# Turning the normalised rows by VectorE squares and DMA through DRAM, in a hybrid decoder layer

## The chip, the cores and the metric

The kernel runs on one core of one Trainium2 chip. Five engines work side by side on that core: TensorE (matmuls), VectorE (DVE), ScalarE (ACT), GpSimd (POOL) and SyncE (SP). In this kernel POOL and SP only issue DMAs, apart from some set-up on POOL. The metric is the device time of one execution in microseconds (us). Timings are compared as medians of several runs.

## The reference

One layer of a decoder, for one sequence of 2048 tokens with 1024 channels, all in fp32:

```python
mod = (silu(c) @ w_ada + b_ada)                 # six vectors: sh1, sc1, g1, sh2, sc2, g2
h = x * (1.0 + sc1) + sh1
z = h @ w_in                                    # 1024 -> 2048 columns
y_conv = gate_b * short_conv(gate_c * v_conv)   # causal, 3 taps
y_pool = multiscale_pool(v_pool)                # means over 2, 4, 8, 16 tokens, then a linear map
mix = concat([y_conv, y_pool]) @ w_out
x = layer_norm(ALPHA * x + (1.0 + g1) * mix, ln1_g, ln1_b)
h = x * (1.0 + sc2) + sh2
f = square(relu(h @ w_mlp_in)) @ w_mlp_out      # 1024 -> 4096 -> 1024
x = layer_norm(ALPHA * x + (1.0 + g2) * f, ln2_g, ln2_b)
```

Between the first layer norm and `h @ w_mlp_in` the layout has to change: the layer norm needs a token on a partition and its channels side by side, the matmul needs a channel on a partition and the tokens side by side. This change of layout is what is edited.

## The kernel before

**Arithmetic.** A fp32 matrix is kept as two parts, `hi` (a cast to the matmul's fp32r format, on ScalarE, line 88) and `lo` (the remainder, a subtraction on VectorE, line 89). `split` makes the pair, and `mm3` (lines 93 to 95) multiplies with three matmuls: hi by hi, hi by lo, lo by hi.

**Blocks.** The sequence is done in two blocks of 1024 tokens (b = 0 and 1). Each block goes through input projection, output projection (`out_proj`) and MLP (`mlp`, with `up` and `down`). The projections use a two-by-two block scheme with seven products instead of eight; which sums of blocks go into which product is in the table `ORDER`, and the operands made from the normalised rows are named by it: "11", "21", "22", "1", "2", "3", "4".

**Output projection.** `out_proj` makes eight tiles `R[0]` to `R[7]` of 128 tokens by 1024 channels. A tile starts as rows of `x` (`load_x`, line 875, on POOL's DMA queue), gets matmul results added in (lines 892 and 899), and is then normalised: statistics on ScalarE (`stats_act`), small steps on both engines (`inv_sqrt`), and last `scale` (line 904), which also stores the tile to the DRAM tensor `nsave` (line 906, POOL's queue), from which `residual` reads it later. Tiles 0 to 3 are complete after `matmuls(4, ...)`, tiles 4 to 7 after `matmuls(6, ...)`. A call of `matmuls` over all four tiles is 48 TensorE matmuls of 128x512, and a product of `up` is 24.

**Turning the rows.** `turned(R)` makes the MLP's operands. Its inner function `transposed(h, k0, dst)` turns the tiles of half h (4h to 4h+3) for the two channel blocks k0 and k0+1: four TensorE transposes of 128x128 into one bank of PSUM (line 773), then an affine with the layer norm's gain and bias (already joined with sc2 and sh2) from PSUM into `dst`, on ScalarE (line 778), or for the second channel block of half 1 on VectorE (line 776). `back(step)` calls it:

```python
if h == 0:
    for q in range(4):
        r = transposed(0, 2 * q, t_r())
        nc.gpsimd.dma_start(hsave[q], r)
        operand("11" if q < 2 else "21", q % 2, r)
```

`back(0)` stands between `matmuls(5, ...)` and `matmuls(6, ...)` and makes "11" and "21" from half 0. `back(1)` stands after the first two products of `up` (g = 0) and turns half 1 into raw tiles. `back(2)`, after the first two products of g = 1, splits "22" from them; `back(3)` to `back(6)` make the other four operands, with tiles read back from `hsave`. The MLP thus begins with products that need half 0 alone: "11", "21", again "11", "21" (g = 1), and the fifth product needs "22".

**What sets the order.** The framework gives each engine and each queue one fixed order when the program is built. It follows the order of the code, except where its own model of the work finds a later instruction ready first; `tc.issue_after(...)` adds an order by hand. So an instruction that has to wait on the chip holds up what is behind it on its engine or queue. Buffers are shared by tag: `o` has 10, `w` 6, `r` 5, `h` 28, `ps` (PSUM banks) 8, and a new tile waits until one of its tag is free.

Of the kernel before, what the change touches and what calls it, by code (L numbers as in the profile page):

```python
# [8 lines left out]
F32 = mybir.dt.float32  # L9
F32R = mybir.dt.float32r  # L10
AF = mybir.ActivationFunctionType
ALU = mybir.AluOpType
# [38 lines left out]
def tile_hybrid_layer(ctx: ExitStack, tc: tile.TileContext, opening, xT, x, wada, win,  # L51
# [29 lines left out]
    def t_ps():  # L81
        return mk(pp, [P, H], F32, "ps", 8)
# [4 lines left out]
    def split(src, hi, lo):  # L87
        high = nc.scalar.copy(hi, src)  # L88
        return high.ins, nc.vector.tensor_tensor(lo, src, hi.bitcast(F32), op=ALU.subtract).ins  # L89


    def mm3(ps, whi, wlo, xhi, xlo, first, last, goes_on=False):
        nc.tensor.matmul(ps, whi, xhi, start=first, stop=False, skip_group_check=goes_on)  # L93
# [97 lines left out]
    msum = tc.dram_tile([7, NG - 1, P, H], F32, name="msum")  # L191
    wosum = tc.dram_tile([2, 4, P, T], F32, name="wosum")
    udeep = tc.dram_tile([NC, P, 3 * Q], F32, name="udeep")
    wdeep = tc.dram_tile([NC, P, T + 3 * Q], F32, name="wdeep")

    def ada_first():
# [562 lines left out]
    def turned(R):  # L759
        B = {}  # L760
        raw = []

        def operand(key, q, src):
            hi, lo = t_h(), t_h()
            split(src, hi, lo)
            B[key, q] = hi, lo

        def transposed(h, k0, dst):
            for i in range(2):
                k = k0 + i  # L770
                ps = t_ps()
                for t in range(4):
                    nc.tensor.transpose(ps[:, t * P : t * P + P], R[4 * h + t][:, k * P : k * P + P], ident)  # L773
                sc, sh = lng[:, k : k + 1], lnb[:, k : k + 1]
                if h and i:
                    nc.vector.tensor_scalar(dst[:, i * H : i * H + H], ps, sc, sh, op0=ALU.mult, op1=ALU.add)
                else:
                    nc.scalar.activation(dst[:, i * H : i * H + H], ps, AF.Identity, bias=sh, scale=sc)
            return dst

        def back(h):
# [5 lines that stand above are left out]
            elif h == 1:  # L787
                for q in range(2):
                    raw.append((transposed(1, 4 + 2 * q, t_o()), transposed(1, 2 * q, t_o())))
            elif h == 2:  # L790
                for q in range(2):
                    operand("22", q, raw[q][0])
            elif h == 3:
                for q in range(2):
                    b11 = t_o()
                    nc.sync.dma_start(b11, hsave[q])
                    tt(raw[q][1], raw[q][1], b11, ALU.subtract)
                    operand("1", q, raw[q][1])
                    raw[q] = raw[q][0], raw[q][1], b11
            elif h == 4:  # L800
                for q in range(2):
                    tt(raw[q][0], raw[q][0], raw[q][1], ALU.subtract)
                    operand("2", q, raw[q][0])
            elif h == 5:
                for q in range(2):
                    tt(raw[q][2], raw[q][0], raw[q][2], ALU.subtract)
                    operand("3", q, raw[q][2])
            else:
                for q in range(2):
                    b21 = t_o()  # L810
                    nc.sync.dma_start(b21, hsave[2 + q])
                    tt(b21, b21, raw[q][0], ALU.subtract)
                    operand("4", q, b21)

        return B, back

# [1 line left out]
    class Operands:  # L820
# [10 lines left out]
        def begin(self, n):  # L831
            i = self.index(n)
            r = t_r()
            nc.sync.dma_start(r.rearrange("p (a n) -> p a n", a=2),
                              msum[i, 0:2].rearrange("a p n -> p a n"))
            self.a[n, 0] = parts(r)
            self.weights(n, 0)

        def weights(self, n, g, tile=None):
# [7 lines left out]
        def second(self, n):  # L847
            ns = range(n, min(n + 2, 7))
            r = t_r()
            for i, m in enumerate(ns):  # L850
                self.a[m, 1] = hi, lo = t_h(), t_h()
                nc.sync.dma_start(r[:, halves[i]], msum[self.index(m), 2])
                split(r[:, halves[i]], hi[:, :H], lo[:, :H])

        def third(self, n):
            hi, lo = self.a[n, 1]
            return split(self.mixed[self.index(n)], hi[:, H:], lo[:, H:])

        def whole(self, n):
            self.begin(n)  # L860
# [2 lines left out]
                self.second(n)  # L863
            self.third(n)

    def out_proj(b, ops):
        R, X, Y = [], {}, {}
        B, back = turned(R)
        lo_, hi_ = halves
        mv = {}  # L870
        late, begun = [], []

        def load_x():
            xt = t_o(D)
            nc.gpsimd.dma_start(xt, x[b * T + len(R) * P : b * T + len(R) * P + P, :])
            R.append(xt)

        def matmuls(n, banks, new, ks, then):
# [23 lines left out]
        def scale():  # L902
            t = late.pop()
            begun[:] = [nc.vector.tensor_scalar(R[t], R[t], mv[t][:, 0:1], mv[t][:, 6:7], op0=ALU.add,
                                                op1=ALU.mult).ins]
            nc.gpsimd.dma_start(nsave[t], R[t])

        def normalise(t):
            stats_act(R[t], mv[t])
# [589 lines left out]
```

## Time and profile before

| | |
|---|---|
| median of 3 runs | 1734.65 us (1734.5 to 1736.54) |
| span of the profiled execution, first to last instruction | 1733.2 us |
| TensorE busy (matmul) | 1723.5 us, 99% |
| VectorE busy | 1314.6 us, 76% |
| ScalarE busy | 868.1 us, 50% |
| POOL busy | 205.8 us, 12% |
| bytes moved by DMA | 465.24 MB, mean 268 GB/s |
| TensorE transposes of normalised rows (line 773) | 128 |

The profile is of one execution; its own time is known as the span, and what lies around the span in a timed run is the difference between the two first rows of the table. In the views, a group row reads: line, engine, operation, out<-in with shapes, count | busy time in us, mean ns of one | idle time of the engine just before them, and what ended it. In the time-ordered views a row starts with start time and duration in us; in brackets stands the idle time of the engine before it and what ended it. In the rows of DMA issues stand the size in KB and the median time from issue to landing in us.

### The profile page before, as it was taken

The numbers are of one execution on the slowest core, as the hardware profiler recorded it, in microseconds if no ns is written. First come the engines' busy times: TensorE is split into PE (matmuls) and PEld (weight loads), VectorE is DVE, ScalarE is ACT, GpSimd is POOL, SyncE is SP. The second block draws the span as 40 slices with busy tenths as digits, with TensorE's granted clock in tenths as the row PEclk, the third lists the DMA queues.
The fourth block names the chain that finished last, engine by engine and source line by source line (L and its number), as shares of the span: only waits on it lengthen the run. The fifth ranks groups of instructions, "written<-read, shape, count | busy, mean of one in ns | idle before, by whom it ended". The sixth has DMA issues, their size and how long they took to land.

```text
span 1733.2 us, 21912 instructions
## 1 busy us (share of the span) xinstructions
PE 1723.5 (99%) x7855; PEld 1435.5 (83%) x7855; DVE 1314.6 (76%) x1726; ACT 868.1 (50%) x1172; POOL 205.8 (12%) x399
## 2 busy tenths in 40 slices
PE   9999999999999999999999999999999999999998
PEld 7888888888888888888888888888888889888887
DVE  8897798877777686669686789687566778665896
ACT  6323368554445554446573344775444567444451
POOL 0222220122322000100000000102111110000000
PEclk9999999999999999999999999999999999999999
DMA  9998877778888998887572366657545589777771
GB/s 387 345 337 319 302 267 269 267 262 325 311 326 319 381 418 332 291 286 284 196 271 76 110 219 219 230 185 282 215 179 222 197 290 418 294 273 249 267 264 50
DMA packets 142685, 465.24 MB, mean 268 GB/s; under 512 B 16488, under 2 KB 17008, under 8 KB 142576
## 3 DMA queue, kind: packets, MB, share of 16 engines
q1 hardware_dynamic: 97920, 303.39, 48.0%
q0 software_dynamic: 44656, 160.46, 24.4%
q8 instruction: 61, 1.00, 0.2%
q14 instruction: 48, 0.39, 0.1%
HBM read 318.55 MB, written 145.23 MB: 268 GB/s over the span
## 4 chain that ended last, share of the span: by engine, by line
PE 95%; DMA 3%; issue 1%; DVE 1%; ACT 0%; SPq 0%; POOL 0%; DVEq 0%; POOLq 0%
PE ps L95 30%; PE ps L93 30%; PE ps L94 30%; PE ps L425 3%; DMA r<-in_w 1%; DMA usum<-o 1%; PE ps L773 1%; DVE o L98 0%; DMA o<-in_w 0%; DMA o<-in_opening 0%; DVE w L89 0%; DVE r L98 0%; ACT w L88 0%; DVE o L1369 0%; SPq L108 0%
## 5 line engine op out<-in xcount | busy, mean ns | idle before, releaser
L95 PE MATMUL ps<-h,w 128*128 128x512 f32 x1312 | 510.2, 389 | 0.4 <-DVE w L89 0.4
L94 PE MATMUL ps<-h,w 128*128 128x512 f32 x1312 | 510.3, 389 | 0.0
L93 PE MATMUL ps<-h,w 128*128 128x512 f32 x1312 | 510.0, 389 | 0.0
L93 PE MATMUL ps<-h,h 128*128 128x512 f32 (+1 forms) x1176 | 444.2, 378 | 0.0
L95 PE MATMUL ps<-h,h 128*128 128x512 f32 (+1 forms) x1176 | 444.1, 378 | 0.0
L94 PE MATMUL ps<-h,h 128*128 128x512 f32 (+1 forms) x1176 | 444.0, 378 | 0.0
L88 ACT CAST h<-r 128x1024 fp32r<-128x1024 f32 (+2 forms) x186 | 187.8, 1014 | 298.0 <-PE ps L94 186.8
L95 PEld LDWEIGHTS ps<-h,w 128*128 128x128 f32 x1312 | 246.3, 188 | 52.1 <-DVE w L89 0.8
L94 PEld LDWEIGHTS ps<-h,w 128*128 128x128 f32 x1312 | 246.3, 188 | 51.5 <-DVE h L89 0.5
L93 PEld LDWEIGHTS ps<-h,w 128*128 128x128 f32 x1312 | 246.0, 188 | 51.3 <-ACT h L88 0.2
L89 DVE TENSOR_TENSOR h<-r,h 128x1024 fp32r<-128x1024 f32 (+2 forms) x186 | 217.3, 1173 | 93.5 <-ACT h L88 93.0
L88 ACT CAST w<-r 128x1024 fp32r<-128x1024 f32 x156 | 164.3, 1053 | 242.6 <-PE ps L94 231.3
L89 DVE TENSOR_TENSOR w<-r,w 128x1024 fp32r<-128x1024 f32 x156 | 190.5, 1222 | 96.3 <-ACT w L88 95.4
L94 PEld LDWEIGHTS ps<-h,h 128*128 128x128 f32 x1176 | 221.3, 188 | 41.1
L95 PEld LDWEIGHTS ps<-h,h 128*128 128x128 f32 x1176 | 221.3, 188 | 40.8
L93 PEld LDWEIGHTS ps<-h,h 128*128 128x128 f32 x1176 | 221.3, 188 | 40.5
L98 DVE TENSOR_TENSOR o<-o,o 128x1024 f32<-128x1024 f32 (+2 forms) x193 | 171.1, 890 | 41.0 <-DMA usum<-o 31.8
L98 DVE TENSOR_TENSOR o<-o,ps 128x512 f32<-128x512 f32 (+1 forms) x175 | 113.7, 658 | 54.3 <-PE ps L95 53.4
L89 DVE TENSOR_TENSOR h<-w,h 128x1024 fp32r<-128x1024 f32 x114 | 137.6, 1207 | 4.3 <-ACT h L88 4.1
L88 ACT CAST h<-w 128x1024 fp32r<-128x1024 f32 x114 | 118.6, 1040 | 12.8 <-DMA w<-wdeep 4.1
L1013 POOL DMA_DIRECT2D usum<-o x111 | 59.4, 535 | 472.3 <-ACT o L1010 195.0
L98 DVE TENSOR_TENSOR r<-r,r 128x1024 f32<-128x1024 f32 x60 | 73.4, 1223 | 21.5 <-DMA r<-in_w 17.5
(160 smaller groups left out, 1243.0 us busy)
## 6 DMA issues: line engine op xcount, KB each, us to landing
usum<-o POOLq DMA_DIRECT2D x111, 512.0 KB, 4.8
r<-usum SPq DMA_DIRECT2D x109, 512.0 KB, 5.5
w<-w2sum SPq DMA_DIRECT2D x64, 512.0 KB, 5.9
r<-in_w SPq DMA_DIRECT2D x60, 512.0 KB, 6.0
w<-in_w SPq DMA_DIRECT2D x40, 512.0 KB, 7.4
o<-in_w SPq DMA_DIRECT2D x72, 256.0 KB, 6.4
w2sum<-o POOLq DMA_DIRECT2D x64, 256.0 KB, 6.7
msum<-o POOLq DMA_DIRECT2D x18, 512.0 KB, 4.9
```

The lines of the kernel that those rows point to most:

```text
L88: high = nc.scalar.copy(hi, src)
L89: return high.ins, nc.vector.tensor_tensor(lo, src, hi.bitcast(F32), op=ALU.subtract).ins
L93: nc.tensor.matmul(ps, whi, xhi, start=first, stop=False, skip_group_check=goes_on)
L94: nc.tensor.matmul(ps, whi, xlo, start=False, stop=False, skip_group_check=goes_on)
L95: nc.tensor.matmul(ps, wlo, xhi, start=False, stop=last, skip_group_check=goes_on)
L98: return nc.vector.tensor_tensor(out_, a, b_, op=op)
L425: nc.tensor.matmul(ps[m, h], wt[:, w : w + P], A[k][p // 2][:, hs], start=k == 0 and p == 0, stop=k == KD - 1 and p == 2)
L773: nc.tensor.transpose(ps[:, t * P : t * P + P], R[4 * h + t][:, k * P : k * P + P], ident)
L1013: nc.gpsimd.dma_start(usum[g, i], r)
```

## The change

TensorE transposes no longer turn the normalised rows. `turn(n)` is called by `scale` for each tile, right after its store to `nsave`. It transposes the tile on VectorE: four instructions of 128x256, each of which turns every 32x32 square by itself, into four gathering tiles `blocks` (tag `w` in half 0, tag `o` in half 1). With the fourth tile of a half, each gathering tile is stored to the new DRAM tensor `tsave` by four DMAs of 32 partitions on POOL's queue, in runs of 128 elements, so that the squares come to lie where a full transpose has them. `transposed` then loads two channel blocks from `tsave` by one DMA on POOL's queue and does the affine in place, its first half on ScalarE, its second on VectorE (for both halves of the rows).

For whole runs of tokens to come out of the squares, a tile `R[t]` holds four groups of 32 tokens that lie 128 apart (`rows_of`). So `load_x` and the store to `nsave` are four DMAs of 32 partitions each in place of one, and the left operands of the output projection are split with their tokens in that order (`split_rows`), in pieces of 512 columns: the 1024-wide split in `begin` becomes two.

```diff
--- before.py
+++ after.py
@@ -88,6 +88,17 @@
         high = nc.scalar.copy(hi, src)
         return high.ins, nc.vector.tensor_tensor(lo, src, hi.bitcast(F32), op=ALU.subtract).ins
 
+
+    def by_rows(ap):
+        return ap.rearrange("p (t a j) -> p a t j", t=4, a=4)
+
+    def by_tokens(ap):
+        return ap.rearrange("p (a t j) -> p a t j", t=4, a=4)
+
+    def split_rows(src, hi, lo):
+        for i in range(0, src.shape[-1], H):
+            cs = slice(i, i + H)
+            split(by_tokens(src[:, cs]), by_rows(hi[:, cs]), by_rows(lo[:, cs]))
 
@@ -191,6 +202,7 @@
     udeep = tc.dram_tile([NC, P, 3 * Q], F32, name="udeep")
+    tsave = tc.dram_tile([2, 4, 2, P, H], F32, name="tsave")
     wdeep = tc.dram_tile([NC, P, T + 3 * Q], F32, name="wdeep")
 
@@ -765,17 +777,30 @@
+        blocks = []
+
+        def turn(n):
+            h, t = n // 4, n % 4
+            if t == 0:
+                blocks[:] = [t_o() if h else t_w(F32) for _ in range(4)]
+            for q, r in enumerate(blocks):
+                nc.vector.transpose(r.rearrange("p (b t j) -> p t b j", b=8, t=4)[:, t],
+                                    R[n][:, q * Q : q * Q + Q].rearrange("p (b j) -> p b j", b=8))
+                if t == 3:
+                    for a in range(4):
+                        own = slice(32 * a, 32 * a + 32)
+                        nc.gpsimd.dma_start(
+                            tsave[h, q].rearrange("k (q i) (a r) -> a i (k q) r", q=4, a=4)[a],
+                            r[own].rearrange("i (b r) -> i b r", b=8))
+
         def transposed(h, k0, dst):
-            for i in range(2):
-                k = k0 + i
-                ps = t_ps()
-                for t in range(4):
-                    nc.tensor.transpose(ps[:, t * P : t * P + P], R[4 * h + t][:, k * P : k * P + P], ident)
-                sc, sh = lng[:, k : k + 1], lnb[:, k : k + 1]
-                if h and i:
-                    nc.vector.tensor_scalar(dst[:, i * H : i * H + H], ps, sc, sh, op0=ALU.mult, op1=ALU.add)
+            nc.gpsimd.dma_start(dst.rearrange("p (k n) -> p k n", k=2), tsave[h, k0 // 2].rearrange("k p n -> p k n"))
+            for i, hs in enumerate(halves):
+                sc, sh = (v[:, k0 + i : k0 + i + 1] for v in (lng, lnb))
+                if i:
+                    nc.vector.tensor_scalar(dst[:, hs], dst[:, hs], sc, sh, op0=ALU.mult, op1=ALU.add)
                 else:
-                    nc.scalar.activation(dst[:, i * H : i * H + H], ps, AF.Identity, bias=sh, scale=sc)
+                    nc.scalar.activation(dst[:, hs], dst[:, hs], AF.Identity, bias=sh, scale=sc)
             return dst
 
@@ -833,7 +858,8 @@
-            self.a[n, 0] = parts(r)
+            self.a[n, 0] = hi, lo = t_h(), t_h()
+            split_rows(r, hi, lo)
             self.weights(n, 0)
 
@@ -850,11 +876,11 @@
-                split(r[:, halves[i]], hi[:, :H], lo[:, :H])
+                split_rows(r[:, halves[i]], hi[:, :H], lo[:, :H])
 
         def third(self, n):
             hi, lo = self.a[n, 1]
-            return split(self.mixed[self.index(n)], hi[:, H:], lo[:, H:])
+            return split_rows(self.mixed[self.index(n)], hi[:, H:], lo[:, H:])
 
@@ -863,16 +889,22 @@
+    def rows_of(t):
+        for a in range(4):
+            start = t // 4 * H + a * P + t % 4 * 32
+            yield slice(start, start + 32), slice(32 * a, 32 * a + 32)
+
     def out_proj(b, ops):
         R, X, Y = [], {}, {}
-        B, back = turned(R)
+        B, back, turn = turned(R)
@@
         def load_x():
             xt = t_o(D)
-            nc.gpsimd.dma_start(xt, x[b * T + len(R) * P : b * T + len(R) * P + P, :])
+            for rs, own in rows_of(len(R)):
+                nc.gpsimd.dma_start(xt[own], x[b * T + rs.start : b * T + rs.stop, :])
             R.append(xt)
@@ -903,7 +935,9 @@
             t = late.pop()
             begun[:] = [nc.vector.tensor_scalar(R[t], R[t], mv[t][:, 0:1], mv[t][:, 6:7], op0=ALU.add,
                                                 op1=ALU.mult).ins]
-            nc.gpsimd.dma_start(nsave[t], R[t])
+            for rs, own in rows_of(t):
+                nc.gpsimd.dma_start(nsave[rs.start // P, rs.start % P : rs.start % P + 32], R[t][own])
+            turn(t)
```

More of the change, by code (lines that the diff above doesn't have):

```diff
@@ L813, in back @@
                     operand("4", q, b21)
-        return B, back
+        return B, back, turn
     class Operands:
```

## Prediction

> **What bounds the kernel now.** I read the page first, for shares, then the groups by form, then windows around the output projection, then the time-ordered views of each engine there.
>
> ```profile
> span 1733.2 us, 21912 instructions
> ...
> PE 1723.5 (99%) x7855; PEld 1435.5 (83%) x7855; DVE 1314.6 (76%) x1726; ACT 868.1 (50%) x1172; POOL 205.8 (12%) x399
> ...
> PE 95%; DMA 3%; issue 1%; DVE 1%; ACT 0%; SPq 0%; POOL 0%; DVEq 0%; POOLq 0%
> ```
>
> TensorE is busy for 99% of the span and carries 95% of the chain that ended last. So time taken off TensorE shortens the run, and any new wait of TensorE lengthens it by as much: the other engines have room to follow. The windows below (columns: length, then busy time and count of PE, PEld, DVE, ACT, POOL, then granted clock, DMA share, GB/s) show the two ends of the output projection, block 0 and block 1, and the end of the run.
>
> ```profile
> 235.00:255.00 20.00, 20.00 (x91) 16.56 (x90) 19.35 (x50) 13.00 (x36) 5.97 (x11) 1.00 0.58 226
> ...
> 1097.00:1112.00 15.00, 14.99 (x83) 12.54 (x82) 7.61 (x16) 10.42 (x15) 2.67 (x5) 1.00 0.56 208
> ```
> ```profile
> 1726.00:1731.00 5.00, 0.00 (x0) 0.00 (x0) 4.06 (x9) 1.18 (x4) 0.00 (x0) 1.00 0.36 143
> 1731.00:1733.20 2.20, 0.00 (x0) 0.00 (x0) 0.00 (x0) 0.00 (x0) 0.00 (x0) 0.53 0.41 153
> ```
>
> TensorE never pauses there. VectorE is full in block 0 (19.35 of 20 us) and half idle in block 1 (7.61 of 15): an added VectorE operation delays block 0 by its own length, block 1 hardly.
>
> **What is removed.**
>
> ```profile
> L773 PE MATMUL ps<-ident,o 128*128 128x128 f32 x128 | 15.6, 275 | 0.0
> ```
> ```profile
> 254.86 2.63 PE ps L773 x24
> ...
> 1101.11 2.63 PE ps L773 x24
> ...
> 1126.69 3.54 PE ps L773 x32
> ```
>
> All 128 TensorE transposes go: four runs of 32 (the first of each block is cut in pieces). An uncut run takes 3.54 us on the chain, 0.11 us each, so **-14.2 us** (4 x 3.54). The 275 ns of the group row are the time of one in a pipeline, and the group's union is only 15.6 us. The Trainium skill (TensorE: Matmul & The Clock Gate, Part 4) gives about 275 ns for such a transpose in a kernel; taken as cost it would make 128 x 0.275 = 35 us of gain, an estimate that these rows contradict.
>
> **When the first product of the MLP can start.** Neighbouring matmuls start 0.2267 us apart: the first and last of 197 rows in a row,
>
> ```profile
> 195.76 0.39 PE L94 MATMUL ps<-h,h 128*128 128x512 f32 x1
> ...
> 240.19 0.39 PE L95 MATMUL ps<-h,h 128*128 128x512 f32 x1
> ```
>
> (44.43 / 196). A `matmuls` call of the output projection is 48 of them, 10.9 us; a product of the MLP 24, 5.44 us. Before, the first run of transposes starts when `matmuls(5)` ends (254.9 and 1101.1); then only `matmuls(6)` is left. After, that call ends and product 0 wants operand "11" at 254.9 + 10.9 = 265.8 and at 1101.1 + 10.9 = 1112.0. Product 0 needs the pair of q=0 at once and that of q=1 six matmuls (1.36 us) later: at 267.2 and 1113.4.
>
> **The new chain to it.** It begins when row 3 is scaled (L904).
>
> ```profile
> 239.93 0.69 DVE L892 SCALAR_TENSOR_TENSOR o<-o,ps 128x512 f32<-128x512 f32 x1 [0.37 <-DMA o<-in_x]
> ...
> 254.05 0.81 DVE L904 TENSOR_SCALAR o<-o,mv 128x1024 f32<-128x1024 f32 x1
> ```
> ```profile
> 1090.26 0.69 DVE L899 SCALAR_TENSOR_TENSOR o<-o,ps 128x512 f32<-128x512 f32 x1 [0.46 <-PE ps L95]
> ...
> 1096.02 0.81 DVE L904 TENSOR_SCALAR o<-o,mv 128x1024 f32<-128x1024 f32 x1 [0.97 <-ACT mv L741]
> ```
>
> In block 1 it ends at 1096.8, in block 0 at 254.9, where the transposes of TensorE already waited for it. Then come 4 VectorE transposes, 4 stores to `nsave`, 16 to `tsave` and 4 loads, all these DMAs on POOL's queue, in the order of the code as I read it, then an affine in two halves, a cast and a subtraction for each q.
>
> ```profile
> L89 DVE TENSOR_TENSOR h<-r,h 128x1024 fp32r<-128x1024 f32 x167 | 203.2, 1221 | 93.3 <-ACT h L88 92.8
> ...
> L98 DVE TENSOR_TENSOR o<-o 128x256 f32<-128x256 f32 x40 | 15.9, 419 | 1.1 <-DMA o<-in_w 0.6 <-ACT o L1054 0.3
> ```
> ```profile
> L356 POOL DMA_DIRECT2D msum<-o x18 | 13.0, 721 | 167.4 <-DVE o L276 105.1 <-DVE o L281 36.6 <-DVE o L98 25.2
> ...
> L906 POOL DMA_DIRECT2D nsave<-o x16 | 8.6, 536 | 57.6 <-DVE mv L750 18.4 <-DVE mv L738 15.2 <-DVE o L904 11.0
> ```
> ```profile
> o<-in_x POOLq DMA_DIRECT2D x16, 512.0 KB, 5.6
> nsave<-o POOLq DMA_DIRECT2D x16, 512.0 KB, 4.1
> ```
> ```profile
> L88 ACT CAST h<-r 128x1024 fp32r<-128x1024 f32 x167 | 175.2, 1052 | 290.3 <-PE ps L94 186.0 <-DMA r<-gout 28.7 <-DMA r<-usum 27.0
> ...
> L778 ACT ACTIVATE r<-ps,lnb,lng 128x512 f32<-128x512 f32 x16 | 11.8, 793 | 7.7 <-PE ps L773 7.7
> ```
>
> No row shows a VectorE transpose. 256 elements per partition should cost near the 0.42 us of an addition of that size; bounds 0.2 (L904 moves 1024 in 0.81) and 0.8. POOL's issue takes 0.536 for the 128 rows of `nsave` and 0.721 for `msum`, as many bytes whose 128 rows go as two runs each, 256 runs. A store to `tsave` is 32 x 8 = 256 runs of 512 B, a load of it 128 x 2 runs, so I take 0.72 for both; bounds 0.53 and twice 0.72, since runs this short are in no row of this queue. Landing: 5.6 us for a 512 KB load on this queue, bounds half and twice that. The landing of the stores costs nothing on the path for q=0 and q=1, as the stores of q=2 and q=3 (8 x 0.72 = 5.8 us) are issued over it; were loads put between stores, it would be paid (4.1 us) but 5.8 us of issue would be saved.
>
> The Trainium skill (DMA: Bandwidth & Descriptors, Anatomy of one DMA) fits 2.0 us plus bytes over 436 GB/s, 3.2 us for 512 KB, as an estimate. By it the sum would be 2 x 2.4 = 4.8 us lower; the 5.6 us row is this queue among this kernel's other traffic, and it decides.
>
> Block 1: scaled 1096.8; `nsave` 4 x 0.53 to 1098.9 (the transposes of q=0, 0.4 us, lie under it); 16 stores x 0.72 to 1110.4; loads issued 1110.4 and 1111.1, landed 1116.0 and 1116.7. ScalarE takes 0.79 + 1.05 for each q (the other half of the affine is on VectorE meanwhile): 1117.8 and 1119.7; the subtraction of q=1 (1.22) ends at 1120.9. Wanted at 1113.4: **+7.5 us**. Bounds: 0 and 25.
>
> Block 0: VectorE is full, so the 12 transposes of rows 0 to 2 (12 x 0.42 = 5.0) push the scaling, and the last `x` tile, for which VectorE waited already at 239.93, now comes as four issues (3 x 0.53 = 1.6 later): scaled at 254.9 + 6.6 = 261.5, 6.6 us after `matmuls(5)` ends where block 1 has it 4.3 us before. The same 24.1 us from there (1096.8 to 1120.9) end at 285.6, wanted at 267.2: **+18.4 us**. Bounds: 5 and 36.
>
> Product 1 takes q=2 and q=3. Loads 3 and 4 land within 5 us of the second, and ScalarE needs 1.84 for each; 5.44 us of product 0 cover it: nothing.
>
> **The second half of the rows** ("22", needed four products, 21.8 us, after product 0). Block 1: product 0 at 1112.0 + 7.5 = 1119.5, "22" wanted at 1141.3 and 1142.6. Row 7 should be scaled 6.6 us after `matmuls(6)` (1090.26 to 1096.83 for row 3), at 1118.6; then 2.1 + 11.5 on POOL, 2.1 for four `hsave` stores in between, loads in the order q=2, 0, 3, 1: the third is issued at 1135.8, lands at 1141.4, is split at 1144.5: **+1.9 us** (bounds 0 and 12). Block 0: TensorE comes 11 us later relative to these rows: nothing.
>
> **The clock.** TensorE pauses 5.8 us in one piece in block 1 (1112.0 to the cast of q=0 at 1117.8), 16.7 in block 0. After 5 us without matmuls the clock at the end of the run falls to half (1731, above), and the opening shows what comes after:
>
> ```profile
> L127 PE MATMUL ps<-o 128*128 128x128 f32 x10 | 2.5, 437 | 1.1 <-DVE o L129 1.1
> ...
> L127 PE MATMUL ps<-ident 128*128 128x128 f32 x6 | 0.8, 275 | 0.0
> ```
>
> the first ten last 437 ns, later ones 275. Some 3 us at half speed cost 1.5 us after each long pause: **+3 us** (bounds 0 and 4).
>
> **Edits at no cost.** 12 more issues for `x` and 12 for `nsave` per block (6.4 us each on POOL, 12% busy; covered by POOL's idle time, except where counted). Halving the seven 1024-wide splits of a block adds about 0.15 us each on ScalarE and VectorE, hidden by TensorE's stream; if writes in runs of 32 elements ran at half speed, 28 splits would cost VectorE and ScalarE up to 19 us a block, spread over 100 us where neither is full save block 0's last 20. `turn` holds four of six `w` buffers in the first half, so weights of products 1 and 2 are split later; TensorE waits then anyway.
>
> **Sum:** -14.2 + 7.5 + 18.4 + 1.9 + 3 = +16.6 on 1733.2, which is 1749.8. The median of the runs is 1734.65, 1.45 above the span: **1751.2 us**.
>
> **Rivals.** (1) The waits stay small: loads are put between the stores and issues go at 0.53. Block 0 then loses some 6 us, block 1 about 1, no clock loss: -14.2 + 7 = -7, 1727.5. For it: VectorE half idle in block 1. Against it: 20 issues of 0.53 are 10.6 us alone, and block 1 has 1113.4 - 1096.8 = 16.6 us for them, a load of 3 to 6 us and 3 us of affine and split. 13 in 100.
> (2) The waits eat the saving, 11 to 18 us together: within 0.2% of before (3.5 us, about what can be told from no change). 12 in 100.
> (3) Slower by more, through one fixed order: ScalarE's affines of the first half stand ahead of the statistics of rows 4 to 7. While ScalarE waits for the loads, four rows of statistics (about 6 us) cannot pass, and the second half, covered in my sum, comes 10 us late in each block: 1751 + 20 = 1771. It decides once the loads land later than the framework's model had them. The same size follows if a store of 256 runs takes POOL 1.4 us (2 x 11). For it: each engine's order is fixed before the run. 21 in 100.
> (4) Transposes free 35 us, by the page quoted: 1751 - 21 = 1730. 2 in 100.
> That the transposes stay or were hidden is excluded: the line is gone, and TensorE has no idle time there to hide them.
>
> **Numbers.** Forecast case 52 in 100. The range takes the Pool and landing bounds of (1) and (3): 1729 to 1785; the forecast's own is 1739 to 1765. Faster 0.15, same 0.12, slower 0.73.
>
> **What would show it.** Waits of TensorE on L88/L89 (operands h), of 7 to 8 us near 1110 and 15 to 20 near 265, preceded by waits of ScalarE on a DMA from `tsave`; POOL rows of `tsave` at 0.72 x 64; VectorE transposes of 0.4 us x 64. A first store issue right after L904 but a last one under 9 us later would make me too high; a TensorE wait before product 5 of over 5 us, or `hsave` stores standing in front of the loads, too low.

## The result, and the profile after

The changed kernel takes 1830.43 us (1828.36 to 1831.78) beside 1734.58 us of the kernel before: a ratio of 1.0546, with an interval of 1.0531 to 1.0561. It is 96 us slower where 16.6 us were forecast. The profiled execution has a span of 1830.0 us.

The page of the changed kernel: the span, the busy times, and the chain that ended last.

```profile
span 1830.0 us, 22027 instructions
...
PE 1723.9 (94%) x7727; PEld 1427.4 (78%) x7727; DVE 1339.1 (73%) x1812; ACT 869.2 (47%) x1178; POOL 301.7 (16%) x575
...
PE 62%; DMA 10%; DVE 7%; issue 4%; POOL 2%; ACT 2%; SPq 0%; DVEq 0%; POOLq 0%; ACTq 0%
```

TensorE is as busy as before (1723.9 us against 1723.5, with 128 transposes fewer), but idle for 6% of the span. The chain, 95% TensorE before, now runs 10% through DMAs. The waits of TensorE by line (what for: total, times, longest, all in us):

```profile
PE ps L104 <- ACT w L88: 52.3, 2, 35.7
PE ps L106 <- DVE w L89: 18.6, 5, 8.7
PE ps L104 <- ACT h L88: 17.7, 4, 8.6
PE ps L105 <- DVE h L89: 4.8, 6, 1.5
...
```

The largest waits end on weights (`w`), not on the operands from the rows (`h`). In order of time on TensorE, at the first product of block 0 and then of block 1:

```profile
301.50 0.80 PE L104 MATMUL ps<-h,w 128*128 128x512 f32 x1 [35.67 <-ACT w L88]
...
311.43 0.80 PE L106 MATMUL ps<-h,w 128*128 128x512 f32 x1 [8.71 <-DVE w L89]
...
1188.85 0.80 PE L104 MATMUL ps<-h,w 128*128 128x512 f32 x1 [16.67 <-ACT w L88]
```

The two kernels issue the same 7,727 other matmuls in one order, so the start of the n-th in one trace less that in the other tells how late it is. By stretches:

| stretch | lateness, us | added | the prediction's term |
|---|---|---|---|
| until `matmuls(6)` of block 0 (one run of transposes gone) | 0 to -3.1 | -3.1 | -3.5 |
| first product, block 0 | -3.1 to 42.5 | +45.6 | +18.4 and half of 3 for the clock |
| second run gone | 42.5 to 39.6 | -2.9 | -3.5 |
| second half of the rows, block 0 | 39.6 to 56.1 | +16.5 | 0 |
| until the end of block 1's `matmuls(5)` (x tile late) | 56.1 to 59.6 | +3.5 | 0 |
| third run gone | 59.6 to 57.0 | -2.6 | -3.5 |
| first product, block 1 | 57.0 to 83.8 | +26.8 | +7.5 and half of 3 for the clock |
| fourth run gone | 83.8 to 80.4 | -3.4 | -3.5 |
| second half of the rows, block 1 | 80.4 to 96.1 | +15.7 | +1.9 |
| to the end | 96.1 to 96.7 | +0.6 | 0 |

The gain came as forecast (-12.0, with small waits in it); each new wait is two to eight times its size or was forecast as nothing. What stands in the line to the first wait, on POOL's queue in block 0 of the changed kernel:

```profile
257.19 2.60 POOL L550 DMA_DIRECT2D w<-in_w  x4
...
273.32 0.57 POOL L557 DMA_DIRECT2D w1sum<-w  x1 [13.03 <-DVE w L109]
...
280.38 9.23 POOL L792 DMA_DIRECT2D tsave<-w  x16 [2.20 <-issue]
...
299.71 0.53 POOL L810 DMA_DIRECT2D hsave<-r  x1 [1.23 <-ACT r L803]
300.31 0.72 POOL L797 DMA_DIRECT2D r<-tsave  x1
```

And on VectorE:

```profile
258.33 0.81 DVE L936 TENSOR_SCALAR o<-o,mv 128x1024 f32<-128x1024 f32 x1
...
272.37 0.65 DVE L109 TENSOR_TENSOR w<-w 128x512 f32<-128x512 f32 x1
```

Row 3 is scaled from 258.3 on (the sum had it done at 261.5), and four transposes later, at 260.6, it is turned. But the 16 stores to `tsave` begin at 280.4: POOL holds them behind the stores of the weight sums, which wait 13 us for VectorE's subtractions, and VectorE has these behind the work on rows 4 to 6. The three first loads go out behind them at 289.6; the fourth stands behind three `hsave` stores until 300.3, and the low part of product 0's weights behind its affine (311.43, above).

What the sums add up is itself loaded late: in the kernel before the same four loads went out 32 us earlier.

```profile
225.21 2.21 POOL L538 DMA_DIRECT2D w<-in_w  x4 [1.80 <-DVE w L211]
```

They go into `w` buffers, and the gathering tiles hold four of the six. The loads go out at 225 in each run below that does not turn half 0 on VectorE, at 257 where only half 0 is turned so, and at 248 to 253 in the kernel before with nothing but VectorE's transposes added. No run gives the gathering tiles buffers of their own, so what this alone costs is not measured.

Block 1 has no weight sums there. POOL, then ScalarE:

```profile
1160.78 4.37 POOL L939 DMA_DIRECT2D nsave<-o  x8 [2.66 <-DVE mv L750]
1165.14 9.66 POOL L792 DMA_DIRECT2D tsave<-w  x16
1174.79 2.15 POOL L797 DMA_DIRECT2D r<-tsave  x3
1183.66 0.59 POOL L810 DMA_DIRECT2D hsave<-r  x1 [6.72 <-DVE r L801]
...
1187.66 0.72 POOL L797 DMA_DIRECT2D r<-tsave  x1
...
1197.35 0.56 POOL L810 DMA_DIRECT2D hsave<-r  x1 [7.51 <-ACT r L803]
...
1208.38 2.35 POOL L792 DMA_DIRECT2D tsave<-o  x4
```
```profile
1179.60 0.81 ACT L803 ACTIVATE r<-r,lnb,lng 128x512 f32<-128x512 f32 x1 [0.39 <-DMA r<-tsave]
1183.21 1.04 ACT L88 CAST h<-r 128x1024 fp32r<-128x1024 f32 x1 [2.80 <-DVE r L801]
...
1187.75 1.04 ACT L88 CAST w<-r 128x1024 fp32r<-128x1024 f32 x1
```

The stores take 9.7 us (forecast 11.5) and the first load lands 4.8 us after its issue (5.6). But the cast of the first operand waits 2.8 us for VectorE's half of the affine, and the cast of product 0's weights comes behind three casts of operands, at 1187.8. The fourth load is issued behind the `hsave` stores; the fourth `hsave` store waits until 1197.4, and the stores of the second half, whose rows were turned by 1182.7 (the last four transposes start at 1181.25 and take 1.42), stand behind it and start at 1208.4.

The clock, in the four windows in which it was granted at half:

```profile
270.00:314.40 44.40, 4.20 (x9) 2.92 (x10) 17.81 (x32) 11.83 (x18) 23.18 (x41) 0.50 0.69 223
338.30:348.50 10.20, 4.78 (x10) 2.86 (x11) 3.96 (x6) 5.49 (x7) 1.34 (x2) 0.50 0.82 321
1174.50:1201.80 27.30, 5.04 (x11) 3.59 (x12) 16.55 (x31) 13.49 (x23) 10.74 (x20) 0.50 0.76 259
1225.70:1236.00 10.30, 5.12 (x10) 3.15 (x11) 4.42 (x7) 5.88 (x8) 0.45 (x1) 0.50 0.84 314
```

These are 40 matmuls (the first count of each row). Where nothing else holds them they start 0.43 us apart in place of 0.23: some 8.0 us, within the terms of the table.

### The profile page after: what moved, and what is told of

Its sections match the earlier page's. It is cut to its first block, busy times and chain, and to the rows that moved or that the text cites. A ratio compares the mean times of both kernels' runs of the same rounds, so it can differ in the third digit from the quotient of the medians.

```text
span 1830.0 us, 22027 instructions
## 1 busy us (share of the span) xinstructions
PE 1723.9 (94%) x7727; PEld 1427.4 (78%) x7727; DVE 1339.1 (73%) x1812; ACT 869.2 (47%) x1178; POOL 301.7 (16%) x575
## 3 DMA queue, kind: packets, MB, share of 16 engines
q1 hardware_dynamic: 97920, 303.39, 46.2%
## 4 chain that ended last, share of the span: by engine, by line
PE 62%; DMA 10%; DVE 7%; issue 4%; POOL 2%; ACT 2%; SPq 0%; DVEq 0%; POOLq 0%; ACTq 0%
PE ps L106 21%; PE ps L105 21%; PE ps L104 21%; DVE o L109 2%; DVE h L89 2%; DMA o<-in_w 1%; DMA r<-tsave 1%; DMA tsave<-o 1%; DMA r<-in_w 1%; DMA usum<-o 1%; POOL tsave L792 1%; DMA o<-tsave 1%; DMA nsave<-o 1%; DVE w L89 1%; POOL nsave L939 1%
## 5 line engine op out<-in xcount | busy, mean ns | idle before, releaser
L88 ACT CAST h<-r 128x1024 fp32r<-128x1024 f32 (+1 forms) x200 | 189.1, 955 | 307.7 <-PE ps L105 194.7
L88 ACT CAST w<-r 128x1024 fp32r<-128x1024 f32 x156 | 164.0, 1052 | 259.7 <-PE ps L105 246.8
L89 DVE TENSOR_TENSOR h<-r,h 128x1024 fp32r<-128x1024 f32 (+1 forms) x200 | 218.3, 1101 | 89.8 <-ACT h L88 89.1
L89 DVE TENSOR_TENSOR w<-r,w 128x1024 fp32r<-128x1024 f32 x156 | 190.4, 1221 | 115.1 <-ACT w L88 113.5
L89 DVE TENSOR_TENSOR h<-w,h 128x1024 fp32r<-128x1024 f32 x114 | 137.5, 1206 | 4.8 <-ACT h L88 4.7
L88 ACT CAST h<-w 128x1024 fp32r<-128x1024 f32 x114 | 118.5, 1040 | 14.6 <-DMA w<-in_w 4.9
```

## The experiments

A result without an interval is one timing of that kernel; the four of the changed kernel lie within 3.4 us of one another.

### Which part costs it

Only tiles 0 to 3 turned in the new way (the others by TensorE), only tiles 4 to 7, and none (rows, pieces and splits stay). In these kernels the affine behind TensorE's transposes writes its result in the order of the tokens. The edit for tiles 0 to 3 alone, with `...` for what is left out; the second run has `h == 0` and `t >= 4` in it, the third `True` and no `turn`:

```diff
         def transposed(h, k0, dst):
+            if h == 1:
+                for i, hs in enumerate(halves):
+                    k, ps = k0 + i, t_ps()
+                    for t in range(4):
+                        nc.tensor.transpose(ps[:, t * P : t * P + P], R[4 * h + t][:, k * P : k * P + P], ident)
+                    sc, sh = (v[:, k : k + 1] for v in (lng, lnb))
+                    if h and i:
+                        nc.vector.tensor_scalar(by_tokens(dst[:, hs]), by_rows(ps), sc, sh, op0=ALU.mult, op1=ALU.add)
+                    else:
+                        nc.scalar.activation(by_tokens(dst[:, hs]), by_rows(ps), AF.Identity, bias=sh, scale=sc)
+                return dst
...
-            turn(t)
+            if t < 4:
+                turn(t)
```

> The mirror: only tiles 0 to 3 go by VectorE and DRAM, tiles 4 to 7 are turned by TensorE. Theory A: both first-half waits stay, 46 and 27 us, less what VectorE gains by not turning tiles 4 to 7 (3 us); 7.1 us of transposes are saved and 4 us of row order paid: 1734 + 73 - 3 - 7 + 4, about 1800 us, and this plus the second run's excess over 1734 gives the 96 us of the whole change within 10. Rival C: the halves do not depend on one another, the first half alone gives half of the loss, about 1780.

Measured 1799.71 us. The number is theory A's, in part by luck: its large waits add up to 62 us and not 70, and the rows cost 20 us and not 4, as the third run shows.

> The kernel after, but only tiles 4 to 7 (half 1) go by VectorE and DRAM; tiles 0 to 3 are turned by TensorE. Theory A: the second half came 16 us late in each block because its stores stood on POOL's queue behind the first half's hsave stores and loads; alone it has 21.8 us of products to hide in, so TensorE waits 0 to 4 us for 22 in each block, 7.1 us of transposes are saved: 1731 to 1742 us. Rival C (the second half's own chain of 36 DMAs is too long even alone): TensorE still waits some 9 us for 22 in each block and runs at half clock after it, 1755 us or more.

Measured 1780.63 us, ratio 1.0265 (1.0250 to 1.0280). TensorE waits 16 us in each block for "22": rival C, with a longer wait. So the second half's trip, in this order of POOL's queue, is too long by itself, without the first in front of it, to be covered by four products.

> The kernel after with its new row order (four DMAs for each tile of x and of nsave, left operands split in the new order) but all rows turned by TensorE again, the affine writing the tokens back in order; no VectorE transposes, no tsave. Theory A (the 96 us are waits of TensorE on the new chain, made long by instructions that stand behind waiting ones in the fixed order of POOL, ScalarE and VectorE): the row order alone costs only what was seen before the chain begins, a wait of 3 us for the last x tile of block 1 and about 1 us elsewhere, so 1736 to 1742 us. Rival B (the reordered splits and the four-fold DMAs slow VectorE, ScalarE and POOL so that rows come late): 15 us or more, 1750 us and over.

Measured 1754.23 us, 1.0119 (1.0102 to 1.0136): 20 us without one row turned in the new way. Theory A fell. So did the other condition of the first run's theory A: the excesses of the two halves add up to 65.3 + 46.2 = 111.5 us and not to 96, as both hold the 20 us of the rows. Above this third run the halves cost 45.5 and 26.4 us, 71.9 of the 76.2 us that both cost together. The next runs look for these 20 us in the kernel before, with the DMAs in pieces, natural order and no other edit:

```diff
-            nc.gpsimd.dma_start(xt, x[b * T + len(R) * P : b * T + len(R) * P + P, :])
+            for a in range(0, P, 32):
+                n = b * T + len(R) * P + a
+                nc.gpsimd.dma_start(xt[a : a + 32], x[n : n + 32, :])
...
-            nc.gpsimd.dma_start(nsave[t], R[t])
+            for a in range(0, P, 32):
+                nc.gpsimd.dma_start(nsave[t, a : a + 32], R[t][a : a + 32])
```

> The kernel before, with the rows of x loaded and the rows for nsave stored in four DMAs of 32 partitions each, in their old order; nothing else is changed. Theory A (the pieces are hidden: POOL is busy 12% of the span, and the 20 us that the new row order cost came from elsewhere, from the split with reordered tokens and from another fixed order of the queues): 1734 to 1738 us. Rival B (the pieces themselves cost it: the last x tile and the buffers come later): 1745 to 1755 us, with waits of TensorE near 282 and 303.

Measured 1753.92 us, 1.0109 (1.0094 to 1.0124): the same 20 us. The pieces make all of them; the reordered splits cost nothing that can be told. SP's queue in this kernel, and the first loads of `hsave` in the kernel before:

```profile
285.79 1.92 SPq L550 DMA_DIRECT2D r<-w1sum  x4
291.95 0.33 SPq L550 DMA_DIRECT2D r<-in_w  x1
294.22 6.69 SPq L550 DMA_DIRECT2D r<-w1sum  x3
301.09 0.84 SPq L796 DMA_DIRECT2D o<-hsave  x1
```
```profile
283.81 1.13 SPq L796 DMA_DIRECT2D o<-hsave  x2
```

The `hsave` loads that make the operand after "22" now stand behind eight loads of weights, 17 us later, and TensorE's longest wait there is 6.8 us, with a half-clock stretch behind it. That the order changed is shown; how much of the delay the buffers of `nsave`'s tiles would have made without it is not.

> The kernel before with the loads of x alone in four pieces of 32 rows; nsave in one DMA per tile as before. Theory A (the pieces' 20 us come mostly from nsave: POOL has more issues to make while rows finish, the buffers come free later, and the loads of weights and of hsave behind them start late): 1736 to 1741 us, the late x tile of each block. Rival B (the pieces of x cost most): 1746 us or more.

> The kernel before with the stores to nsave alone in four pieces of 32 rows; x in one DMA per tile as before. Theory A (nsave makes most of the 20 us, through buffers that come free late): 1746 to 1753 us. Rival B (the pieces of x make it): 1735 to 1741.

Measured 1741.99 (1.0044, 1.0029 to 1.0059) and 1742.10 us (1.0042, 1.0025 to 1.0059). Neither theory holds: the kinds cost 7.5 and 7.6 us, and both together 19.6, more than the sum.

The kernel before with VectorE's 64 transposes into tiles that nothing reads (`turn` as in the change, without its stores):

> The kernel before, with the 64 VectorE transposes of the change added into gathering tiles that nothing reads: no store, no load, TensorE turns as before. Theory A (the step of the prediction: block 0 pays about 5 us, block 1 with VectorE half idle next to nothing): 1736 to 1742 us. Rival B (the transposes stand in the chain from row to row in both blocks, 1.35 to 1.7 us a row): 1744 to 1752.

Measured 1737.75 us, 1.0019 (1.0010 to 1.0028). Theory A met: VectorE's work is the cheap part, 3.5 us.

### What is the trip through DRAM, and what its order

The changed kernel without stores to and loads from `tsave`; the affines read the gathering tiles, so that the channels of a square stay in wrong places:

```diff
-            nc.gpsimd.dma_start(dst.rearrange("p (k n) -> p k n", k=2), tsave[h, k0 // 2].rearrange("k p n -> p k n"))
+            src = blocks[k0 // 2]
...
-                    nc.scalar.activation(dst[:, hs], dst[:, hs], AF.Identity, bias=sh, scale=sc)
+                    nc.scalar.activation(dst[:, hs], src[:, hs], AF.Identity, bias=sh, scale=sc)
```

> The changed kernel without the trip through DRAM: no stores to tsave and no loads, the affines read the gathering tiles, so the channels of a square stay in wrong places and the output is another; VectorE transposes, row order, pieces, affines and splits all stay. Theory A (the trip, its issues, landings and what waits in line with it, makes nearly all of the 96 us beyond the pieces' 20): 1737 to 1752 us, that is 1734.4 + 20 for the pieces + 3 for VectorE - 14 for TensorE, with 5 either way. Rival B (VectorE and the fixed orders around the turn hold much of it): 1770 us or more.

Measured 1764.76 us, 1.0173 (1.0156 to 1.0190), between the two: the trip is worth 65.7 us, and 30 remain. In this kernel the operands are split by 269 us in block 0 (last subtraction of L89 on `h` at 268.23, 1.22 long), and TensorE waits 8.0 and 5.8 us at 274 and 282 for the first product's weights. Their load had landed by 246.6; ScalarE casts them behind the statistics of the rows, and VectorE subtracts behind the weight sums and rows 4 to 6:

```profile
272.96 1.03 ACT L88 CAST w<-r 128x1024 fp32r<-128x1024 f32 x1
```
```profile
280.60 1.21 DVE L89 TENSOR_TENSOR w<-r,w 128x1024 fp32r<-128x1024 f32 x1
```

POOL's queue there holds up the weights of the next products:

```profile
280.52 2.66 POOL L804 DMA_DIRECT2D hsave<-r  x4 [2.42 <-ACT mv L748]
283.17 2.44 POOL L933 DMA_DIRECT2D nsave<-o  x5
287.73 0.49 POOL L933 DMA_DIRECT2D nsave<-o  x1 [2.11 <-DMA hsave<-r]
289.02 0.49 POOL L933 DMA_DIRECT2D nsave<-o  x1 [0.80 <-DMA hsave<-r]
291.16 0.49 POOL L933 DMA_DIRECT2D nsave<-o  x1 [1.66 <-DMA hsave<-r]
292.54 0.49 POOL L933 DMA_DIRECT2D nsave<-o  x1 [0.88 <-DMA nsave<-o]
```

The `hsave` stores, which free the `r` buffers that the weights are loaded into, go only at 280.5, behind the weight sums' stores. Next, both orders of the weights mended in this kernel:

```diff
+        if b == 0:
+            sum_weights(w1[0], w1sum[0], lambda w: t_w(F32), begun[0], halves[1 : 2])
         matmuls(4, Y, False, every, first_row)
-        if b == 0:
-            sum_weights(w1[0], w1sum[0], lambda w: t_w(F32), begun[0], halves[1 : 2])
...
+        W = summed_weights(w1[0], w1sum[0], (0, 1, 7, 4, 5, 6, 3))
+        first = parts(next(W), t_w)
         back(0)
```

`up` then takes `W` and `first` for its first products. The weight sums are of block 0 alone; the first weights are made early in both blocks, here and in every run below that has this edit.

> The run without the trip through DRAM (1764.8 us), with the weight sums and the first weights of block 0 early as well; the output is another, as there. Theory A (what is left there in block 0 is the weights, held up by w buffers and by the stores in front of the ones that free their buffers): the first product of block 0 loses its waits, 10 to 15 us less, 1748 to 1755 us. Rival B (VectorE's turn and the statistics hold it): 1760 us or more.

Measured 1751.69 us, 1.0099 (1.0084 to 1.0114): 13.1 us less, theory A. So the 96 us are a ladder of three steps between measured kernels, in this order of taking away (with the trip in place the same two edits are worth 10 us, below): 1734.5 to 1751.7 (pieces and VectorE's turn less TensorE's transposes), to 1764.8 (weights in their old place), to 1830.4 (the trip). The first step, 17.2 us, is more than its parts measured singly (19.6 + 3.5 - 14.2 = 8.9); TensorE still waits there twice for weights, 6.2 and 5.5 us, and which edit makes these two waits stays open.

The same mending in the changed kernel with its trip, first both edits, then each alone:

> The changed kernel with two fixed orders of block 0 undone: the weight sums of w1 are all made ahead of the fifth product of the output projection, and the first weights of the MLP are split before the turned rows are. Theory A (in block 0 the waits of 36 and 9 us are half the chain of DMAs, as in block 1 with 17 and 8.5, and half these orders): 15 to 22 us less than the changed kernel, 1808 to 1815. Rival B (the chain of stores and loads alone makes the wait): at most 5 us less, 1825 to 1830.

Measured 1820.30 us, 10 less; between the two. The first product of block 0 gained 19 us, but TensorE's waits for "22" behind it grew from 8.1 and 8.6 us to 15.6 and 16.5.

> The changed kernel with the second half of the weight sums made ahead of the fifth product of the output projection, and nothing else. Theory A (POOL holds 16 tsave stores behind four w1sum stores that wait 13 us for VectorE, so this order alone delays the first product of block 0): the wait of 36 us shortens by 10 to 20 us, but the weights are then split behind the operands, so the total falls by 5 to 12 us, 1818 to 1825. Rival B (the order of the first weights is what counts): 1828 us or more.

Measured 1815.05 us, 15.4 less: a little over theory A's gain. The wait of 36 us became 21.4.

> The changed kernel with the first weights of the MLP split ahead of the turned rows, in both blocks, and the weight sums where they were. Theory A (the stores behind w1sum set the first wait; the weights come 1 us behind the operands, and only the second wait, 8 to 9 us in each block, can go): 1815 to 1826 us. Rival B (the weights are worth nothing once the operands are late): 1828 us or more.

Measured 1831.64 us: rival B. The first wait of TensorE now ends on `h` in place of `w` and is nearly as long, 31.5 us, and the waits for "22" grew here too, to 15.6 and 14.9. So the row "ACT w L88 35.7" named what came last, not what made the wait. POOL's wait for the sums made 14 us of it, as the run before shows; the other 21 are the trip and what stands in line with it. Both edits together (10 us) are worth less than the sums alone (15.4).

The `hsave` stores from ScalarE's queue, alone and then with both edits of the weights:

```diff
-                    nc.gpsimd.dma_start(hsave[q], r)
+                    nc.scalar.dma_start(hsave[q], r)
```

> The kernel after, with the four hsave stores of each block issued from ScalarE's queue in place of POOL's, where they stood in front of the fourth load from tsave and of the stores of rows 4 to 7. Theory A: the fourth load goes out with the others, so the second wait of TensorE (8.5 to 9 us for the low part of the first weights, behind the affine of that load) shrinks to 2 or less, and the second half's stores go out some 10 us earlier: 12 to 18 us less per block, 1795 to 1806 us. Rival D (the fourth load was late because its r buffer was taken, and the second half because of the landing of the DMAs before it): within 6 us of 1830.

Measured 1818.89 us, 11.5 less: between the two. The fourth load now goes out 3 us after the first instead of 11 and 13.

> The changed kernel with the edits of two earlier runs together: weight sums and first weights of block 0 early (alone 10 us less), and the stores to hsave from ScalarE's queue (alone 11.5 us less). Theory A (they mend different waits, one the order of the weights in block 0, one the stores in front of the last load): 1806 to 1812 us. Rival B (they mend the same wait): 1815 to 1820.

Measured 1799.11 us, 31.3 less: better than theory A, the best of these kernels with the trip in both halves, and still 65 above the kernel before. About a third of the 96 us was order alone.

`nsave` behind the `tsave` stores (`turn(t)` first, and the pieces of all four rows with the fourth):

> The changed kernel with the 16 pieces of a half for nsave issued behind its tsave stores, in place of row by row ahead of them. Theory A (POOL issues one DMA after the other, and what stands ahead of the tsave stores delays them; 4.4 us of pieces do so in the first half of block 1, more in the second halves): 1805 to 1820 us. Rival B (the rows, not POOL, are late, or the pieces only move in front of the loads): 1825 to 1835.

Measured 1824.01 us, 6.4 less: just below rival B, above theory A.

Two of the four gathering tiles stored from ScalarE's queue:

```diff
-                        nc.gpsimd.dma_start(
+                        (nc.scalar if q > 1 else nc.gpsimd).dma_start(
                             tsave[h, q].rearrange("k (q i) (a r) -> a i (k q) r", q=4, a=4)[a],
```

> The changed kernel with half of the tsave stores (those of the third and fourth gathering tile) from ScalarE's queue. Theory A (16 stores of 0.6 us one behind the other on POOL are the longest part of the chain): 4.8 us less in each half of each block, about 1811 to 1818 us. Rival B (the stores' landing or VectorE sets it, or ScalarE's queue has its own order in the way): 1825 us or more.

Measured 1813.37 us, 17.1 less: inside theory A's range, but not by its equal parts. The first product of block 0 came out 13 us better and the second halves 6 and 7, the first product of block 1 3 us worse: ScalarE issues eight stores from 1149.8 to 1158.6 there, and its statistics of rows 4 to 7 start only then.

All mendings at once:

> The changed kernel with all mendings at once: weight sums and first weights of block 0 early, hsave from ScalarE's queue, half of the tsave stores from ScalarE's queue, nsave behind the tsave stores. Theory A (each shortens a part of one line of DMAs that stays in front of TensorE; the pieces, the trip of the second half and the landings remain): 1772 to 1795 us. Rival B (the orders were all of it, the trip can be hidden): under 1750. Rival C (ScalarE's queue clogs instead): 1800 or more.

Measured 1825.99 us, 1.0530 (1.0515 to 1.0546): rival C. ScalarE in this kernel, with its queue:

```profile
264.49 7.36 ACTq L792 DMA_DIRECT2D tsave<-w  x8
272.06 0.72 ACT L764 ACTIVATE tmp<-o,mv 128x512 f32<-128x512 f32 x1 [10.14 <-DMA tsave<-w]
```

Issues take 0.92 us each there, and ScalarE's own work stands still for 10 us until they are out; at 299.7 three more take 9.4 us, and in block 1, at 1185.8, seven take 19.9 us while its own work stands for 18.9. Mendings that help one by one do not add up once they share a queue. No version beat the kernel before.

The last run joins the four pieces of a tile to one DMA again, in the new row order (four runs of 32 rows on the DRAM side):

```diff
+            t = len(R)
+            rows = x[b * T + t // 4 * H : b * T + t // 4 * H + H, :].rearrange("(a q j) d -> q a j d", a=4, q=4)
+            nc.gpsimd.dma_start(xt, rows[t % 4])
...
+            rows = nsave[t // 4 * 4 : t // 4 * 4 + 4].rearrange("a (q j) d -> q a j d", q=4)
+            nc.gpsimd.dma_start(rows[t % 4], R[t])
```

> The changed kernel with one DMA per tile, of 128 partitions, for the rows of x and for nsave, in the new row order, in place of four. Theory A (POOL's queue sets the chain: some 3 us of issues fewer ahead of the tsave stores in each half of each block): 1810 to 1818 us. Rival B (rows, landings and VectorE set it, the issues lie beside them): 1825 to 1831.

Measured 1875.74 us, 1.0813 (1.0790 to 1.0837): 45 us slower where both theories had it faster or equal. The DMA issues of this kernel, then of the changed one (size, median us to landing):

```profile
o<-in_x POOLq DMA_DIRECT2D x16, 512.0 KB, 14.9
nsave<-o POOLq DMA_DIRECT2D x16, 512.0 KB, 15.6
```
```profile
o<-in_x POOLq DMA_DIRECT2D x64, 128.0 KB, 6.2
nsave<-o POOLq DMA_DIRECT2D x64, 128.0 KB, 4.5
```

The issues did fall to a quarter in number, at 0.69 and 0.71 us each, but each DMA lands after 15 us. In block 0 VectorE now waits 4.5 and 5.8 us for tiles of `x` at 245 and 260, and TensorE comes to product 0 36 us late, where in the changed kernel it came early. The Trainium skill (DMA: Bandwidth & Descriptors, "Why a DMA increments its semaphore by 16 and not by 1") states that a DMA uses the largest number of DMA engines, up to 16, that divides the size of the slowest dimension on both of its sides; by that it is 4 here, and 16 for 128 rows or 32. The traces agree: in this kernel, while the load of `x` issued at 1107.4 is alone on POOL's queue, at most 4 of its 128 packets are under way at once; in the kernel before, during the store to `nsave` issued at 1089.4, it is mostly 16.

## Why the prediction was wrong

**Direction and place were right.** VectorE's transposes take 0.41 us (0.42 taken), a store's issue 0.59 (0.72), a load's issue 0.72 (0.72), the first landing 4.8 and 5.4 (5.6), and the transposes of TensorE gave back their 12 to 14 us. The chance for slower, 0.73, stood; rivals 1, 2 and 4, which had the waits small or the gain large, fell. Both signs that it named for being too low came: TensorE waits 8.1 and 8.6 us before product 5, and `hsave` stores stand in front of a load.

**The term "+18.4, block 0" measured 45.6.** The step that failed is "the same 24.1 us from there": the DMAs were taken to go out "in the order of the code". POOL's queue had stores of weight sums ahead of `tsave`, and they waited 13 us for VectorE. In the code itself the second call of `sum_weights` stands ahead of the `scale()` of row 3, so the reading of the order passed over it; and the working gave the gathering tiles four of six `w` buffers and counted only the weights of products 1 and 2, not the sums, which use `w` too. The run with the sums alone moved took 14 us off this wait, and with it the first product of block 0 costs some 33 us. The bound of 36 left that queue out.

**The term "+7.5, block 1" measured 26.8.** The row was scaled 6 us later than taken (1161.87 against 1096.02, less the 59.6 us by which TensorE was late): "block 1 hardly" was wrong, as VectorE's transposes alone move row 3 there by 3.2 us against the end of `matmuls(5)`, and the pieces of `x` alone by 3.2. Two rows of `nsave` stood ahead instead of one (0.4 us), and "ScalarE takes 0.79 + 1.05 for each q" forgot who shares the operand: VectorE's half of the affine came 2.8 us late, behind rows 6 and 7, and the weights were cast behind three operands. Then 8 us more for the fourth load. Of this the sentence "loads 3 and 4 land within 5 us of the second" was wrong by its own warning: `hsave` stands in front of the loads.

**"Nothing" and "+1.9" for the second half measured 16.5 and 15.7.** The working had the stores of half 1 at 1118.6 + 2.1 + 2.1. In the trace they wait 26 us on POOL's queue in block 1 (turned 1182.7, first store 1208.4), behind an `hsave` store that waits for ScalarE, and 13 pieces of `nsave`. Even without the first half in front (the run with tiles 4 to 7 alone) the wait was 16 us. Rival 3 had a mechanism of this kind, one fixed order that makes the second half 10 us late in each block, but the one that it named did not act: ScalarE's statistics of rows 4 to 7 ran ahead of the affines (1176.6 and 1179.6 in block 1). POOL's order did.

**"Edits at no cost" cost 19.6.** The cover named was POOL's idle time, and POOL is indeed idle, 84% of the span. But the x tiles come later by the pieces, and SP's order moved; the share of the buffers is not shown. The idle share of an engine says nothing on what stands behind one of its instructions.

**"TensorE waits then anyway" for the weights cost 13**, as far as the run without the trip shows. There the operands are ready and the weights are not.

**"+3" for the clock measured some 8.0**, as four stretches were slowed and not two, each by 2 us and not 1.5.

## What to carry to other kernels

Before a step is moved to DMA, write down, for each queue it will use, the instructions ahead of it and what each of these waits for, and who else uses the buffers that it takes; here mending that order alone took 31 of 96 us off. A pause that ends on a weight can be made by an operand, and the reverse: only moving one of them tells. Cutting a DMA in four is not free on a queue that is idle most of the time (19.6 us here), and joining it over four far-apart runs can be worse.

## What the runs showed of the hardware

A DMA issue on POOL takes about as long for 32 rows as for 128: 0.49 to 0.51 us for a quarter of a tile of `x` or `nsave` (492 and 508 ns on average) against 0.54 for a whole one, and 0.60 for 256 runs of 512 B; a whole tile over four far-apart runs of rows took 0.69 to 0.71. POOL does not issue without limit: in the rows of POOL in the run without the trip, the tenth of a series waits for the second to land (`hsave`, three waits in a row), then the `nsave` pieces follow, as if eight could be under way at a time; whether the queue or the framework sets this is not shown. Quarter pieces reach that with a quarter of the bytes. A DMA with four runs of rows as its slowest dimension landed in 15 us instead of 4 to 6, and where it was alone at most 4 of its packets were under way at once. And ScalarE, asked to issue 8 stores of 256 runs, took 5.3 to 9.2 us where they went out in a row, in the two runs that have them, and hardly did any of its own work meanwhile.
